# Weight blocks' transfers on GpSimd's queue, and an earlier "free" time in the planner of a two-layer hybrid decoder

## The chip, the cores and the metric

The kernel runs on one core of a Trainium2 chip. Such a core has a matrix engine (TensorE, PE in the profile; PEld is its loading of weights), a vector engine (VectorE, DVE), a scalar engine (ScalarE, ACT), GpSimd (POOL) and SyncE (SP), which here only issues transfers. Each engine has its own program and runs it in order; engines wait for each other at semaphores. Sixteen DMA engines move data between DRAM and the on-chip memory (SBUF); an engine that issues a transfer goes on at once, unless the transfer's own semaphores hold it. The metric is the time of one execution in microseconds on the device, the median of several; lower is better.

## The reference

Two layers, 528 tokens (16 learned meta tokens and 512 real ones), width 1024, float32. Each layer is a mixer and a feed-forward part:

```python
u = rms_norm(h, pre_g)
z = einsum("bld,de->ble", u, w_in)              # q, k, v, forget gate, conv value/gate, sc_b, sc_c, sc_x
y_attn = forgetting_attention(q, k, v, log_f)   # 8 heads of 64, causal softmax with summed log gates
a = causal_depthwise_conv(a_val * sigmoid(a_gate), a_dw_w) + a_dw_b      # 31 taps, 256 channels
y_conv = einsum("blc,ce->ble", silu(layer_norm(a)), a_pw_w)
y_sc = sc_b * causal_depthwise_conv(sc_c * sc_x, sc_conv_w)              # 3 taps, 256 channels
y = head_rms_norm(concat[y_attn, y_conv, y_sc], head_g)
h = h + rms_norm(y @ w_out, post_g)

z = causal_depthwise_conv(rms_norm(h, pre_g) @ w_up, conv_w)             # width 2 x 2816
g, up = split(z)
h = h + rms_norm((silu(g) * up) @ w_down, post_g)
```

The output is h without the meta tokens.

## The kernel before

Tokens lie along the free axis, in two halves of 264 columns; channels lie on 128 partitions, so that h is 8 tiles of 128 x 528. Matrix products keep float32's accuracy by splitting each operand into a high and a low part of a faster format: `mm3` (line 658) issues three matmuls per product, high x high, low x high and high x low. Each weight block, 128 x 1024 as a rule, is therefore loaded raw from DRAM (line 610, 512 KB), rounded to its high part on ACT (line 614), and its low part is the difference on DVE (line 618). There are three raw buffers and a few rings of buffers for the parts. Some weight blocks of layer 1 are prepared during the feed-forward part of layer 0: their parts are written to DRAM (`split_w`), and later fetched as a pair of transfers, high and low (line 626).

The stages are the front (norm of the input and the first half of layer 0's first projection), the mixer of each layer, and each sub-layer's end. Inside a mixer, the projections (`proj`, with the split input uhi and ulo, line 1852 and on), the attention of eight heads and the two convolution branches are interleaved. For a pair of heads, scores are first taken for their row maxima (line 1389, DVE reduces them, line 1396), the maxima go as an extra row into q (line 1416), scores are computed again (line 1435), ACT takes the exponential p (line 1444), POOL zeroes the part above the diagonal (`affine_select`, line 1451), DVE sums (line 1460), and `weighing` (line 1481) multiplies by the values. Odd heads need q and k on other partitions; these are small copies between SBUF tiles issued on SP by the helper `dma` at line 525, as are forget-gate sums through DRAM (`g_dram`, into rows of k).

The convolution branch (tiles apad, cacc) has 31 taps on DVE (line 974), a norm over channels, silu, and a pointwise product (a_pw_w). The short branch (cxp, sccx) has three taps. Each 128-channel tile of the concatenated result then has a head norm: ACT squares it (line 1157), a matmul with a block-diagonal matrix (bd) sums the squares (line 1163), ACT makes the reciprocal root (lines 1128, 1131, 1132), DVE refines it (1133, 1136) and scales (1147), ACT casts the high part (1150) and DVE forms the low one (1151). The output projection with w_out follows; its sums go out at line 1680 with the squares of the next norm at line 746. In the front, the norm's factors rs and rz come from squares (line 746), sums on DVE (755), a matmul (795), ACT (805 to 809) and DVE (810, 816); DVE scales h with them at line 1848.

What sets the order of all this is a planner, `Flow`. Every operation is entered with its engine, an estimated time (0.17 + 0.0009 n us on ACT, 0.17 + 0.00101 n on DVE for n columns; transfers by their bytes), a priority, the operations that it waits for and the buffers that it takes. `Flow.run` walks through a planned time: it takes, again and again, the engine or TensorE thread that can start first, emits its instruction, and sets when that engine is free and when the result is there. So the order of the instructions of each engine, TensorE's matmuls included, is the order in which the plan reaches them. The weight loads are such operations on the engine "sp", whose planned queue they share with the small copies. The inner stretch of the feed-forward part is written without the planner, with loads of its own on SP (lines 473, 494 and 499).

Of the kernel before, what the change touches and what calls it, by code (L numbers as in the profile page):

```python
# [9 lines left out]
F32 = mybir.dt.float32  # L10
# [5 lines left out]
P = 128  # L16
# [19 lines left out]
FIRST = {"w_out": 4, "ffn_w_down": 6}  # L36
# [12 lines left out]
LATE = 6  # L49

WARM, WARM_US = 20, 5.6


_COLS = {}
# [49 lines left out]
def chunk_cols(c):  # L104
    return sum(n for _, n in c[4])
# [102 lines left out]
class Flow:  # L208
# [59 lines left out]
    def run(self, stop=None):  # L268
        while True:
            if stop is not None and stop():  # L270
                return
            best = None
            for eng, ops in self.pend.items():
                can = [(r + self.HOP, o) for o in ops if (r := self.ready(o[4], o[7])) is not None]
                if can:
                    start = max(self.free[eng], min(r for r, _ in can))
                    o = min((o[0], r, o[1], o) for r, o in can if r <= start)[3]
                    if o[0] >= self.yields:
                        soon = [(r, q[0], q[1], q) for r, q in can if q[0] < o[0] - 0.5 and r < start + 0.6 * o[2]]
                        if soon:  # L280
                            start, _, _, o = min(soon)
                    if best is None or start < best[0]:
                        best = (start, eng, o)
            can = [(r, i) for i, t in enumerate(self.threads) if (r := self.ready(t[1])) is not None]
            if can:
                start = max(self.pe, min(r for r, _ in can))
                if best is None or start < best[0]:
                    best = (start, None, self.threads[min(i for r, i in can if r <= start)])
            if best is None:
                assert not self.threads and not any(self.pend.values()), "nothing can go on"  # L290
                return
            start, eng, o = best
            self.now = start
            if eng is not None:
                self.pend[eng].remove(o)
                _, _, us, fn, _, tok, lat, _, takes = o
                for r, slot in takes:
                    r.take(slot)
                fn()
                self.free[eng] = start + us  # L300
                tok.time = start + us + lat
                continue
            self.pe = max(self.pe, start)
            try:
                y = next(o[0])
            except StopIteration:
                self.threads.remove(o)
                continue
            o[1] = [Tok(0.0)] if y is None else [Tok(self.pe + y)] if isinstance(y, float) else y
# [7 lines left out]
def act_us(n):  # L317
    return 0.17 + 0.0009 * n


def dve_us(n):
    return 0.17 + 0.00101 * n


def stt_us(n):
    return 0.22 + 0.00102 * n


def dma_us(n):

    return max(0.35, n * P * 4 / 400e3)


def dma_lat(n):

    return 1.0 + 0.00234 * n
# [3 lines left out]
def tile_hybrid_trunk(ctx: ExitStack, tc: tile.TileContext, xT, wflat, pv_d, out):  # L340
    nc = tc.nc
# [3 lines left out]
    def T(pool, shape, dt, tag, bufs=None):  # L345
        uid[0] += 1
        kw = {} if bufs is None else {"bufs": bufs}
        return pool.tile(list(shape), dt, tag=tag, name=f"{tag}_{uid[0]}", **kw)
# [70 lines left out]
    flow = Flow()  # L419
# [23 lines left out]
    offs = []  # L443
# [13 lines left out]
    def wtile(i, tag):  # L457
        if chunks[i][0] == "a_pw_w":
            if tag == "whi":
                pw_place[0] = pw_place[0]()  # L460
            n = chunks[i][3] * chunk_cols(chunks[i])
            return pw_place[0][:, :n] if tag == "whi" else pw_place[0][:, n:2 * n]
        return T(wx[0], [P, WCHUNK], F32R, tag) if i in wide else T(wp, [P, CHUNK], F32R, tag)
# [19 lines left out]
    for i in ahead:  # L483
        sz = chunks[i][3] * chunk_cols(chunks[i])
# [30 lines left out]
    def act(us, fn, *after, **kw):  # L515
        return flow.op("act", us, fn, after, **kw)

    def dve(us, fn, *after, **kw):
        return flow.op("dve", us, fn, after, **kw)
# [53 lines left out]
    raws = Ring(3)  # L573
    split = {"rot": Ring(3), "wide": Ring(WIDE), "pw": [Ring(1) for _ in range(DEPTH)]}
    coming = deque()
    fetched, filled = [], []
# [18 lines left out]
    def plan_w(limit, prio=2):  # L595

        for i in range(wpos[0], min(limit, len(chunks))):
            plan_block(i, prio)
        wpos[0] = max(wpos[0], min(limit, len(chunks)))

    def plan_block(i, prio):
        kn, n = chunks[i][3], chunk_cols(chunks[i])
        sz = kn * n
        b = Block()
        box = {}
        slot = Slot()

        def load():
            box["raw"] = T(wp, [P, CHUNK], F32, "raw", 3)
            nc.sync.dma_start(box["raw"][:, :sz], wflat[offs[i]:offs[i] + P * sz].rearrange("(p s) -> p s", p=P))  # L610

        def high():
            box["hi"] = wtile(i, "whi")
            nc.scalar.copy(box["hi"][:, :sz], box["raw"][:, :sz])  # L614

        def low():
            lo = wtile(i, "wlo")
            nc.vector.tensor_sub(lo[:, :sz], box["raw"][:, :sz], box["hi"][:, :sz].bitcast(F32))  # L618
            b.w = tuple(t[:, :sz].rearrange("p (k n) -> p k n", n=n) for t in (box["hi"], lo))

        ring = split["pw"][chunks[i][1]] if chunks[i][0] == "a_pw_w" else split["wide" if i in wide else "rot"]
        if i in home:
            def fetch():
                ws = wtile(i, "whi"), wtile(i, "wlo")
                for t, d in zip(ws, (home[i][0], home[i][1])):
                    nc.sync.dma_start(t[:, :sz].bitcast(F32), d[:, :sz])
                b.w = tuple(t[:, :sz].rearrange("p (k n) -> p k n", n=n) for t in ws)

            b.tok = flow.op("sp", 2 * dma_us(sz), fetch, filled, prio=prio, lat=dma_lat(sz), takes=[(ring, b.slot)])
            fetched[:] = [b.tok]  # L630
            coming.append((i, b))
            return

        got = flow.op("sp", dma_us(sz), load, prio=prio, lat=dma_lat(sz), takes=[(raws, slot)])
        a = act(act_us(sz), high, got, *fetched, prio=prio, takes=[(ring, b.slot)])
        filled[:] = [a]
        b.tok = dve(dve_us(sz), low, a, prio=prio)
        slot.close(b.tok)
        coming.append((i, b))
# [27 lines left out]
    def two(t):  # L667
        return t.rearrange("p (a b) -> p a b", a=2)
# [1143 lines left out]
    with tc.tile_pool(name="pre", bufs=2, reuse_waits="tile") as sp, tc.manual_schedule(engines=every):  # L1812
# [13 lines left out]
        for k in range(KD):  # L1826
# [3 lines left out]
            d = dve(stt_us(H), lambda hk=hk, hi=hi, lo=lo, gc=gc: nc.vector.scalar_tensor_tensor(  # L1830
                lo, in0=hk, scalar=gc, in1=hi.bitcast(F32), op0=ALU.mult, op1=ALU.subtract), c, prio=0)
# [46 lines left out]
    for l in range(DEPTH):  # L1878
# [21 lines left out]
        with tc.tile_pool(name=f"fp{l}", bufs=2, reuse_waits="tile") as fp:  # L1900
# [78 lines left out]
            for part, nf in enumerate(PARTS):  # L1979
# [14 lines left out]
                if part < len(PARTS) - 1:  # L1994
                    for m in range(KD):
                        w = next_w()
                        ps = mmt()
                        if final:

                            mm3({0: ps[:, 0, :2 * fw]}, w, ks, lambda b, k, hf, f0=f0: g[f0 + k][b][:, :2 * fw])  # L2000
                            d, src = yp[:, m, t0:], ps[:, 0, :2 * fw]
                        else:
                            mm3({hf: ps[:, hf, :fw] for hf in range(2)}, w, ks, grhs)
                            d, src = two(yp[:, m, t0:]), ps[:, :, :fw]
# [69 lines left out]
```

## Time and profile before

| | us |
|---|---|
| median of 3 runs | 1304.11 |
| lowest, highest | 1301.64, 1304.61 |
| the profiled execution, its own time | 1301.54 |
| its span in the trace | 1299.8 |
| ACT busy | 612.6 (47%) |
| small groups left out of the page, busy | 1424.2 |

The profile has 24250 instructions. The granted clock of TensorE has a mean of 0.995 of full speed. Busy time is a sum over instructions of an engine; a row of waits names the instruction that waited and what released it last. Matmuls overlap in TensorE's pipeline: a single one lasts longer in the trace than the distance to the next. A row such as `L658` is the line of the kernel before; `SPq` and `POOLq` are the issuing of transfers by those engines.

### The profile page before, as it was taken

The page shows a single profiled execution, that of the slowest core. Times are in us where ns is not written, and L with a number is a line of the kernel's source. Part 1 is how long each engine was busy: PE and PEld are TensorE (multiplying, and loading weights), DVE is VectorE, ACT ScalarE, POOL GpSimd, SP SyncE. Part 2 cuts the span into 40 slices and gives each one's busy share as a digit, 9 for nine tenths or more (in the row PEclk, how much of TensorE's full clock was granted, in tenths as well). Part 3 has the DMA queues.
Part 4 walks back from the last instruction along what each step waited for, and adds up shares of the span by engine and source line. Part 5 has one row for each costly group of instructions (what it writes and reads, how often), then busy time and mean ns, then how long its engine had stood idle before and what let it go on. Part 6 is the DMA issues. An engine that isn't in the chain of part 4 may idle for free. (4 is left out here: it accounts for less than half of the span.)

```text
span 1299.8 us, 24250 instructions
## 1 busy us (share of the span) xinstructions
PE 1273.3 (98%) x9922; PEld 1217.7 (94%) x9922; DVE 895.1 (69%) x1563; ACT 612.6 (47%) x1144; POOL 58.8 (5%) x166
## 2 busy tenths in 40 slices
PE   8999999999999999999999899999999999999997
PEld 8988888999999999999999798889999799989997
DVE  7888896688734774677568786756876256636664
ACT  7255567655433442444552344676543234314453
POOL 1310100000000000000003111100000000000000
PEclk9999999999999999999999999989999999999999
DMA  7032213516554556654742353234033323232321
GB/s 238 34 101 84 81 54 101 190 56 205 203 173 157 192 199 223 227 195 146 241 158 68 116 164 123 74 118 145 18 98 97 97 85 94 72 116 91 92 72 65
DMA packets 56335, 164.56 MB, mean 127 GB/s; under 512 B 6352, under 2 KB 16720, under 8 KB 56224
## 3 DMA queue, kind: packets, MB, share of 16 engines
q1 hardware_dynamic: 56176, 162.88, 38.7%
q8 instruction: 78, 1.28, 0.4%
q14 instruction: 33, 0.27, 0.1%
q0 software_dynamic: 48, 0.13, 0.0%
HBM read 131.17 MB, written 27.46 MB: 122 GB/s over the span
## 5 line engine op out<-in xcount | busy, mean ns | idle before, releaser
L658 PE MATMUL psum<-uhi,whi 128*128 128x264 f32 (+1 forms) x1936 | 452.8, 287 | 1.3 <-ACT uhi L1852 0.8
L658 PE MATMUL psum<-ulo,whi 128*128 128x264 f32 (+1 forms) x1936 | 445.5, 284 | 0.6 <-DVE ulo L1854 0.4
L658 PE MATMUL psum<-uhi,wlo 128*128 128x264 f32 (+1 forms) x1936 | 445.2, 284 | 0.0
L658 PEld LDWEIGHTS psum<-uhi,whi 128*128 128x128 f32 x1936 | 322.8, 189 | 3.9 <-ACT uhi L1852 1.0
L658 PEld LDWEIGHTS psum<-ulo,whi 128*128 128x128 f32 x1936 | 322.4, 188 | 1.9 <-DVE ulo L889 0.6
L658 PEld LDWEIGHTS psum<-uhi,wlo 128*128 128x128 f32 x1936 | 322.7, 189 | 0.0
L658 PE MATMUL psum<-yhi,whi 128*128 128x264 f32 (+3 forms) x888 | 250.4, 305 | 6.4 <-ACT yhi L1150 2.1
L658 PE MATMUL psum<-ylo,whi 128*128 128x264 f32 (+3 forms) x888 | 247.6, 301 | 1.0 <-DVE ylo L1151 1.0
L658 PE MATMUL psum<-yhi,wlo 128*128 128x264 f32 (+3 forms) x888 | 247.6, 301 | 0.8 <-DVE wlo L618 0.8
L475 ACT CAST whi<-raw 128x1024 fp32r<-128x1024 f32 (+1 forms) x110 | 113.1, 1030 | 182.9 <-PE psum L658 145.0
L476 DVE TENSOR_TENSOR wlo<-raw,whi 128x1024 fp32r<-128x1024 f32 (+1 forms) x110 | 131.7, 1199 | 65.5 <-ACT whi L475 63.7
L658 PEld LDWEIGHTS psum<-yhi,whi 128*128 128x128 f32 x888 | 160.8, 191 | 15.1 <-ACT yhi L1150 3.5
L658 PEld LDWEIGHTS psum<-ylo,whi 128*128 128x128 f32 x888 | 161.0, 190 | 7.5 <-DVE ylo L1151 1.9
L658 PEld LDWEIGHTS psum<-yhi,wlo 128*128 128x128 f32 x888 | 161.2, 190 | 6.7 <-DVE wlo L618 1.4
L1955 DVE SCALAR_TENSOR_TENSOR c<-z,pv,c 128x528 f32<-128x528 f32 (+1 forms) x176 | 131.9, 756 | 2.7
L618 DVE TENSOR_TENSOR wlo<-raw,whi 128x1024 fp32r<-128x1024 f32 (+2 forms) x64 | 75.6, 1196 | 28.0 <-ACT whi L614 27.7
L974 DVE SCALAR_TENSOR_TENSOR cacc<-apad,pv,cacc 128x528 f32<-128x528 f32 x120 | 87.5, 763 | 1.0
L614 ACT CAST whi<-raw 128x1024 fp32r<-128x1024 f32 (+2 forms) x64 | 64.7, 1028 | 25.9 <-PE psum L658 15.1
L1965 ACT ACTIVATE c<-c 128x528 f32<-128x528 f32 (+1 forms) x44 | 28.1, 639 | 83.7 <-DVE c L1955 83.6
L1973 ACT CAST yhi<-c 128x528 fp32r<-128x528 f32 (+1 forms) x44 | 27.5, 626 | 84.2 <-DVE c L1969 84.2
L1953 ACT ACTIVATE c<-z,pv 128x528 f32<-128x528 f32 (+1 forms) x88 | 63.4, 727 | 0.1
L1921 DVE TENSOR_TENSOR z<-psum,rz 128x250 f32<-128x250 f32 x80 | 30.4, 420 | 46.5 <-PE psum L658 46.4
(220 smaller groups left out, 1424.2 us busy)
## 6 DMA issues: line engine op xcount, KB each, us to landing
raw<-in_w_dram SPq DMA_DIRECT2D x160, 512.0 KB
raw<-in_w_dram SPq DMA_DIRECT2D x32, 448.0 KB
split_w<-whi SPq DMA_DIRECT2D x20, 512.0 KB
split_w<-wlo SPq DMA_DIRECT2D x20, 512.0 KB
whi<-split_w SPq DMA_DIRECT2D x20, 512.0 KB
wlo<-split_w SPq DMA_DIRECT2D x20, 512.0 KB
h<-in_x_dram SPq DMA_DIRECT2D x16, 264.0 KB
q<-q SPq DMA_DIRECT2D x16, 132.0 KB
```

The source lines that it names most:

```text
L475: nc.scalar.copy(hi[:, :sz], raw[:, :sz])
L476: nc.vector.tensor_sub(lo[:, :sz], raw[:, :sz], hi[:, :sz].bitcast(F32))
L614: nc.scalar.copy(box["hi"][:, :sz], box["raw"][:, :sz])
L618: nc.vector.tensor_sub(lo[:, :sz], box["raw"][:, :sz], box["hi"][:, :sz].bitcast(F32))
L658: nc.tensor.matmul(d, lhsT=w[a][:, k, cols], rhs=rhs(b, k, hf), start=start and i == 0 and p == 0, stop=stop and i == n - 1 and p == 2)
L974: nc.vector.scalar_tensor_tensor(conv[j], in0=src, in1=conv[j], scalar=col("a_dw_w", CK * j + i), op0=ALU.mult, op1=ALU.add)
L1921: nc.vector.tensor_mul(t[:, off + a - i0:off + z - i0], src, rz[:, a:z])
L1953: nc.scalar.activation(dst, src[:, 2:2 + 2 * fw], AF.Copy, scale=wtap(2, t))
L1955: nc.vector.scalar_tensor_tensor(dst, in0=src[:, i:i + 2 * fw], scalar=wtap(i, t), in1=dst, op0=ALU.mult, op1=ALU.add)
L1965: silu = nc.scalar.activation(cs[0], cs[0], AF.Silu)
L1973: nc.scalar.copy(ghi, cs[0])
```

## The change

Three things change. First, the transfers of all weight blocks from block 6 on (both the raw loads and the fetched pairs, in both layers' planned stages) are issued by GpSimd, on a planned engine of their own, "wdma"; each pushes the planner's free time of "pool" on by 0.75 us. The first six raw loads, the small copies, the loads of h and the feed-forward part's own loads stay on SP. Of the issues, 104 change their engine: 60 raw loads and 44 halves of fetched pairs. Second, the raw loads on the new queue wait in the plan for the last load on SP (`behind`). Third, after an operation the planner sets its engine free 0.09 us earlier than the operation's estimated end (for operations under 0.18 us, at half of it); transfers' queues are left out of this, and the time at which a result is there stays as it was. The lines behind the change are numbered higher, by 1 at first, by 11 around line 620, and by 13 from line 650 on (so line 1451 becomes 1464, and 1163 becomes 1176).

```diff
--- before.py
+++ after.py
@@ -49,6 +49,7 @@
 LATE = 6
 
 WARM, WARM_US = 20, 5.6
+GP_DMA = 0.75
 
 
 _COLS = {}
@@ -297,7 +298,7 @@
                 for r, slot in takes:
                     r.take(slot)
                 fn()
-                self.free[eng] = start + us
+                self.free[eng] = start + (us if eng in ("sp", "wdma") else max(us - 0.09, 0.5 * us))
                 tok.time = start + us + lat
                 continue
             self.pe = max(self.pe, start)
@@ -598,16 +599,26 @@
             plan_block(i, prio)
         wpos[0] = max(wpos[0], min(limit, len(chunks)))
 
+    behind = []
+
     def plan_block(i, prio):
         kn, n = chunks[i][3], chunk_cols(chunks[i])
         sz = kn * n
         b = Block()
         box = {}
         slot = Slot()
+        queue = "wdma" if i >= FIRST["ffn_w_down"] else "sp"
+
+        def bring(to, src):
+            if queue == "sp":
+                nc.sync.dma_start(to, src)
+                return
+            flow.free["pool"] = max(flow.free.get("pool", 0.0), flow.now) + GP_DMA
+            nc.gpsimd.dma_start(to, src)
 
         def load():
             box["raw"] = T(wp, [P, CHUNK], F32, "raw", 3)
-            nc.sync.dma_start(box["raw"][:, :sz], wflat[offs[i]:offs[i] + P * sz].rearrange("(p s) -> p s", p=P))
+            bring(box["raw"][:, :sz], wflat[offs[i]:offs[i] + P * sz].rearrange("(p s) -> p s", p=P))
 
         def high():
             box["hi"] = wtile(i, "whi")
@@ -623,15 +634,17 @@
             def fetch():
                 ws = wtile(i, "whi"), wtile(i, "wlo")
                 for t, d in zip(ws, (home[i][0], home[i][1])):
-                    nc.sync.dma_start(t[:, :sz].bitcast(F32), d[:, :sz])
+                    bring(t[:, :sz].bitcast(F32), d[:, :sz])
                 b.w = tuple(t[:, :sz].rearrange("p (k n) -> p k n", n=n) for t in ws)
 
-            b.tok = flow.op("sp", 2 * dma_us(sz), fetch, filled, prio=prio, lat=dma_lat(sz), takes=[(ring, b.slot)])
+            b.tok = flow.op(queue, 2 * dma_us(sz), fetch, filled, prio=prio, lat=dma_lat(sz), takes=[(ring, b.slot)])
             fetched[:] = [b.tok]
             coming.append((i, b))
             return
 
-        got = flow.op("sp", dma_us(sz), load, prio=prio, lat=dma_lat(sz), takes=[(raws, slot)])
+        got = flow.op(queue, dma_us(sz), load, behind if queue == "wdma" else (), prio=prio, lat=dma_lat(sz), takes=[(raws, slot)])
+        if queue == "sp":
+            behind[:] = [got]
         a = act(act_us(sz), high, got, *fetched, prio=prio, takes=[(ring, b.slot)])
         filled[:] = [a]
         b.tok = dve(dve_us(sz), low, a, prio=prio)
```

The order of SP's issues in the mixer of layer 1, where the copies of the odd heads' q and k are made (q and k are copies between tiles, whi and wlo the fetched pair of a weight block), was:

```order
L525 DMA q_767_7988<-q_766_7987 64x528
L525 DMA q_769_7990<-q_768_7989 64x528
L626 DMA whi_8305<-split_w_114 128x1024
L626 DMA wlo_8306<-split_w_114 128x1024
L626 DMA whi_8336<-split_w_114 128x1024
L626 DMA wlo_8337<-split_w_114 128x1024
L525 DMA k_759_7980<-k_758_7979 64x528
L525 DMA k_761_7982<-k_760_7981 64x528
L626 DMA whi_8450<-split_w_114 128x1024
L626 DMA wlo_8451<-split_w_114 128x1024
```

and is now, at the same copies:

```order
L526 DMA q_767_7990<-q_766_7989 64x528
L526 DMA q_769_7992<-q_768_7991 64x528
L526 DMA k_759_7982<-k_758_7981 64x528
L526 DMA k_761_7984<-k_760_7983 64x528
L526 DMA k_758_7981<-g_dram_21_113 1x528 x2
L526 DMA k_760_7983<-g_dram_21_113 1x528 x2
L526 DMA q_771_7994<-q_770_7993 64x528
L526 DMA q_773_7996<-q_772_7995 64x528
```

The fetched pairs are gone from between the copies, which follow each other. On POOL, in the same mixer, what stands between the last clearing of buffers and the first causal selects (p, a head's exponentials) is now:

```order
L617 DMA whi_8176<-split_w_114 128x1024
L617 DMA wlo_8177<-split_w_114 128x1024
L617 DMA whi_8212<-split_w_114 128x1024
L617 DMA wlo_8213<-split_w_114 128x1024
L617 DMA whi_8269<-split_w_114 128x1024
L617 DMA wlo_8270<-split_w_114 128x1024
L617 DMA whi_8344<-split_w_114 128x1024
L617 DMA wlo_8345<-split_w_114 128x1024
L1464 AFFINE_SELECT p_776_8015<-p_776_8015 128x128 x4
L1464 AFFINE_SELECT p_776_8015<-p_776_8015 16x16
L617 DMA whi_8472<-split_w_114 128x1024
L617 DMA wlo_8473<-split_w_114 128x1024
```

Before, the selects followed the clearing with no transfer between them; now four pairs stand ahead of the first select, and a fifth pair between those of two heads.

At the end of the mixer of layer 0 TensorE's rows from the last two sums of squares of the head norms (L1163; apad holds squares of the convolution branch, yhi and ylo are the normed tiles that the output projection reads) were:

```order
L1163 MATMUL psum_67<-apad_2666,bd_93 128x264
L1163 MATMUL psum_67<-apad_2665,bd_93 128x264
L658 MATMUL psum_67<-yhi_292_2681,whi_2238 128x264
L658 MATMUL psum_67<-ylo_293_2682,whi_2238 128x264
L658 MATMUL psum_67<-yhi_292_2681,wlo_2299 128x264
L658 MATMUL psum_67<-yhi_292_2681,whi_2432 128x264
L658 MATMUL psum_67<-ylo_293_2682,whi_2432 128x264
L658 MATMUL psum_67<-yhi_292_2681,wlo_2471 128x264
L658 MATMUL psum_67<-yhi_294_2693,whi_2238 128x264
L658 MATMUL psum_67<-ylo_295_2694,whi_2238 128x264
L658 MATMUL psum_67<-yhi_294_2693,wlo_2299 128x264
L658 MATMUL psum_67<-yhi_294_2693,whi_2432 128x264
```

and from the last two sums of squares now (L1176; cxp holds squares of the short branch):

```order
L1176 MATMUL psum_67<-cxp_2650,bd_93 128x264
L671 MATMUL psum_67<-yhi_140_1156,whi_2262 128x264
L671 MATMUL psum_67<-ylo_141_1157,whi_2262 128x264
L671 MATMUL psum_67<-yhi_140_1156,wlo_2269 128x264
L671 MATMUL psum_67<-yhi_140_1156,whi_2515 128x264
L671 MATMUL psum_67<-ylo_141_1157,whi_2515 128x264
L671 MATMUL psum_67<-yhi_140_1156,wlo_2545 128x264
L1176 MATMUL psum_67<-cxp_2650,bd_93 128x264
L671 MATMUL psum_67<-yhi_158_1357,whi_2262 128x264
L671 MATMUL psum_67<-ylo_159_1358,whi_2262 128x264
L671 MATMUL psum_67<-yhi_158_1357,wlo_2269 128x264
L671 MATMUL psum_67<-yhi_158_1357,whi_2515 128x264
```

Before, the convolution branch's norms came last, and the matmuls right behind the last sums read their result: the first use of a second half of it is the thirteenth matmul. Now the short branch's norm is last, and tiles with finished norms are read first: between the first of the two sums and the first use of its tile (yhi_297) are 42 matmuls of the output projection, between the second and its use 78.

In the front, ACT's rows from the second half's norm factor (rs) to the first casts of the scaled input (uhi; sccx and cxp are the gates of the convolution branch here, whi a weight block) were:

```order
L805 ACTIVATE rs_47_176<-psum_67,c_rms_101 128x264
L808 ACTIVATE rs_47_176<-rs_47_176 128x264
L809 ACTIVATE rs_47_176<-rs_47_176 128x264
L935 ACTIVATE sccx_140<-sccx_140 128x264
L935 ACTIVATE cxp_144<-cxp_144 128x264
L937 ACTIVATE sccx_140<-sccx_140,c_one_99 128x264
L937 ACTIVATE cxp_144<-cxp_144,c_one_99 128x264
L938 ACTIVATE sccx_140<-sccx_140 128x264
L938 ACTIVATE cxp_144<-cxp_144 128x264
L1852 CAST uhi_106<-h_175 128x2x264
L614 CAST whi_437<-raw_340 128x1056
L1852 CAST uhi_106<-h_175 128x2x264 x5
```

and are now:

```order
L818 ACTIVATE rs_47_176<-psum_67,c_rms_101 128x264
L821 ACTIVATE rs_47_176<-rs_47_176 128x264
L948 ACTIVATE sccx_140<-sccx_140 128x264
L822 ACTIVATE rs_47_176<-rs_47_176 128x264
L950 ACTIVATE sccx_140<-sccx_140,c_one_99 128x264
L1865 CAST uhi_106<-h_175 128x2x264
L951 ACTIVATE sccx_140<-sccx_140 128x264
L948 ACTIVATE cxp_144<-cxp_144 128x264
L1865 CAST uhi_106<-h_175 128x2x264
L950 ACTIVATE cxp_144<-cxp_144,c_one_99 128x264
L625 CAST whi_415<-raw_331 128x1056
L1865 CAST uhi_106<-h_175 128x2x264
```

The casts of uhi now begin among the gates' rows, and the weight block's cast stands behind the second of them.

## The prediction

> **What bounds the kernel now.** I read the page's busy shares first, then the busy time in windows of 50 us, then TensorE's waits, then the timeline around each wait that is longer than a third of a microsecond.
>
> ```profile
> PE 1273.3 (98%) x9922; PEld 1217.7 (94%) x9922; DVE 895.1 (69%) x1563; ACT 612.6 (47%) x1144; POOL 58.8 (5%) x166
> ```
>
> TensorE (PE) is busy for 1273.3 of 1299.8 us, so all that a change of order and of queues can win is its 26.5 us of idle time. No matmul is added or taken away by the diff. The windows (stretch, its length, then busy us and instructions of PE, weight load, DVE, ACT, POOL, the granted clock, the DMA share, GB/s) show where the idle time lies:
>
> ```profile
> 200.00:250.00 50.00, 47.33 (x366) 45.42 (x365) 28.68 (x48) 33.06 (x70) 0.27 (x4) 1.00 0.47 149
> 350.00:400.00 50.00, 50.00 (x412) 50.00 (x411) 18.29 (x20) 16.37 (x23) 0.00 (x0) 1.00 0.44 141
> 700.00:750.00 50.00, 45.01 (x352) 40.41 (x351) 38.19 (x93) 17.27 (x50) 4.39 (x12) 0.97 0.38 122
> 850.00:900.00 50.00, 48.16 (x359) 45.98 (x359) 28.18 (x47) 31.92 (x64) 0.00 (x0) 0.93 0.49 156
> ```
>
> The feed-forward part (350 to 400) has no idle time: one matmul per 50 / 412 = 0.121 us. Only the mixers and their ends lose time: 2.67 us in 200 to 250, 4.99 in 700 to 750, 1.84 in 850 to 900. TensorE's waits (us in total, times, longest) name what came last:
>
> ```profile
> PE psum L1435 <- DMA k<-k: 3.5, 1, 3.5
> PE psum L658 <- ACT yhi L1150: 2.1, 2, 1.5
> PE psum L658 <- ACT whi L614: 2.0, 1, 2.0
> ...
> PE psum L658 <- DVE ylo L1151: 1.0, 3, 0.4
> ...
> PE psum L1435 <- ACT q L1416: 0.9, 1, 0.9
> PE psum L658 <- ACT uhi L1852: 0.8, 1, 0.8
> ...
> PE psum L658 <- ACT acc L746: 0.5, 1, 0.5
> ...
> PE psum L658 <- DVE ulo L1854: 0.4, 1, 0.4
> ```
>
> The longest is a small copy of one head's keys. The next three kinds are the head norms at the end of a mixer (L1150, L1151), and the first weight block, which stays on SP and which I leave at 2.0. Weight transfers are otherwise hidden.
>
> **The change part by part.** *The keys' copy, mixer 1.* These are SP's issues ahead of it, PE's matmul that waited, and the sizes:
>
> ```profile
> 718.73 0.55 SPq L626 DMA_DIRECT2D whi<-split_w  x1
> ...
> 720.33 0.39 SPq L626 DMA_DIRECT2D wlo<-split_w  x1
> 720.82 1.36 SPq L525 DMA_DIRECT2D k<-k  x2
> ```
> ```profile
> 728.70 1.21 PE L1435 MATMUL psum<-q,k 128*128 128x16 f32 x5 [3.54 <-DMA k<-k]
> ```
> ```profile
> whi<-split_w SPq DMA_DIRECT2D x20, 512.0 KB
> ...
> k<-k SPq DMA_DIRECT2D x16, 132.0 KB
> ```
>
> Four transfers of 512 KB stand directly ahead of two of 132 KB, and the matmul that needs the first copy starts at 728.70, 7.9 us after its issue. These 2.3 MB in the 10 us from 718.73 to 728.70 are some 230 GB/s: the copy waited behind weights. In the new order SP holds nothing but small copies there, and the four fetches stand on POOL. If the copies no longer queue behind 2 MB, they land 2 to 4 us after issue (an estimate: their own 0.26 MB at 230 GB/s is 1.1 us, and the one transfer on POOL's queue, row below, took 4.0 with its fixed part); PE had been ready 3.54 us before 728.70, which is 4.3 us after the issue. Bounds: 0 if the engines still serve them in order of issue, 3.5 if not, and below nothing if they get worse, which I exclude since the bytes around them are the same. I take **3.5**, nearest to the 4.3 us of room. The rule that speaks against it is in the Trainium skill, "DMA: Bandwidth & Descriptors", section "Issuing engines are not separate DMA queues": DMAs of all issuers run on the same 16 engines and interleave, so that another issuer saves only the time to issue. By it the 3.5 would shrink towards nothing; its section "Queues, rings and completion order" has each engine alternate between queue rows packet by packet, by which a short copy would take its half share and pass. No run here shows two rows at once, so both stay.
>
> *The end of each mixer.* PE's, then ACT's rows around the last head norm of mixer 0, then PE's waits in mixer 1:
>
> ```profile
> 213.91 1.05 PE L1163 MATMUL psum<-apad,bd 128*128 128x264 f32 x4
> ...
> 215.68 0.39 PE L658 MATMUL psum<-ylo,whi 128*128 128x264 f32 x1 [0.38 <-DVE ylo L1151]
> ...
> 218.39 0.41 ACT L1150 CAST yhi<-cacc 128x264 fp32r<-128x264 f32 x1 [0.94 <-DVE cacc L1147]
> ...
> 218.85 0.51 PE L658 MATMUL psum<-yhi,whi 128*128 128x264 f32 x2 [1.48 <-ACT yhi L1150]
> ```
> ```profile
> 860.41 1.52 PE L1163 MATMUL psum<-apad,bd 128*128 128x264 f32 x4 [0.61 <-DVE rs_t L1133]
> ...
> 862.83 0.43 PE L658 MATMUL psum<-ylo,whi 128*128 128x250 f32 x1 [0.39 <-DVE ylo L1151]
> ...
> 866.01 0.81 PE L658 MATMUL psum<-yhi,whi 128*128 128x264 f32 x2 [0.62 <-ACT yhi L1150]
> ```
>
> From the end of the last statistics matmul (213.91 + 1.05 = 214.96) to the cast of its result (218.39 + 0.41) are 3.8 us. In the old order 12 matmuls, 1.5 us at 0.121, stand between those matmuls and the first that uses a second half; hence the waits. In the new order the convolution's pointwise product and norm come before the short convolution's, and the last norm's first half has 42 output-projection matmuls (5.1 us) and its second 78 (9.4 us) before their use. 5.1 and 9.4 both exceed 3.8, the first by only 1.3, which two extra ACT rows in between take up. Gain: 0.38 + 1.48 + 0.3 (the two smaller waits in mixer 0 have 1.0 in three with mixer 1's 0.39 and 0.38) = 2.1, and 0.61 + 0.39 + 0.62 = 1.6 in mixer 1: **3.7**, bounds 2 and 4.5. The 0.5 for acc L746, a wait for a PSUM buffer to be read out, I leave.
>
> *The opening.* PE's two waits, and ACT's rows before them:
>
> ```profile
> 31.01 0.39 PE L658 MATMUL psum<-uhi,whi 128*128 128x264 f32 x1 [0.77 <-ACT uhi L1852]
> 31.77 0.39 PE L658 MATMUL psum<-ulo,whi 128*128 128x264 f32 x1 [0.37 <-DVE ulo L1854]
> ```
> ```profile
> 26.14 0.41 ACT L935 ACTIVATE sccx<-sccx 128x264 f32<-128x264 f32 x1
> 26.45 0.41 ACT L935 ACTIVATE cxp<-cxp 128x264 f32<-128x264 f32 x1
> ...
> 28.21 0.62 ACT L1852 CAST uhi<-h 128x528 fp32r<-128x528 f32 x1
> ...
> 30.32 0.63 ACT L1852 CAST uhi<-h 128x528 fp32r<-128x528 f32 x1 [0.52 <-DVE h L1848]
> ```
>
> Six small rows (26.14 to 28.21) and a weight cast stand ahead of the first two casts of u; in the new order the first cast follows two of them, that weight cast comes behind the second cast of u, and DVE scales three tiles of h ahead of the second half's factor instead of none. I count both waits as gone: **1.1**, bounds 0 and 1.1, since the earlier norm matmuls may wait 0.2 to 0.4 themselves.
>
> *Restart.* After a wait PE's next matmul starts later than 0.121 us behind (31.01 shows 0.39 of one matmul, against 0.28 to 0.29 in a running stream), some 0.1 for each of the ten waits counted: **1.0**.
>
> *The planner's rule.* The two L935 rows start 0.31 us apart though each lasts 0.41: an engine really starts the next operation some 0.1 before the end of one. The old plan spaces such a row at 0.17 + 0.0009 x 264 = 0.41, the new one at 0.32. So the new plan is near the chip and without slack; where an operation starts later than planned, PE has less work placed ahead. I put **1.5 back** (some ten dense places of the mixers at 0.15, the 0.1 of a row and a half), bounds 0 and 10 (ten at the 1.0 of the larger waits above).
>
> *POOL's queue.* 104 issues (60 raw loads, 44 halves of prepared blocks) move to POOL. These rows are POOL's group for its one old transfer and its landing, its causal selects, its own waits, DVE's waits for the selects, and SP's for a free block:
>
> ```profile
> L378 POOL DMA_DIRECT2D pv<-in_pv_dram x1 | 0.7, 668 | 0.8 <-POOLq L2065 0.8
> ```
> ```profile
> pv<-in_pv_dram POOLq DMA_DIRECT2D x1, 127.0 KB, 4.0
> ```
> ```profile
> L1451 POOL TENSOR_SCALAR_AFFINE_SELECT p<-p 128x128 f32<-128x128 f32 (+1 forms) x80 | 30.1, 388 | 234.9 <-ACT p L1444 234.0
> ```
> ```profile
> POOL p L1451 <- ACT p L1444: 234.0, 43, 31.9
> ...
> ACT whi L614 <- DMA raw<-in_w_dram: 10.1, 12, 2.0
> ...
> DVE psum L1460 <- POOL p L1451: 6.2, 10, 3.2
> ```
>
> At 0.668 us, 104 issues are 69 us on an engine busy for 58.8 of 1299.8: no load of its own. Both have 128 rows of one partition each, so I take 0.668; were the time to grow with bytes it would be 512 / 127 x 0.668 = 2.7 us each, 280 us in all. What matters is order: behind a weight transfer that waits for its buffer stand the next causal selects, and behind those DVE's sums and PE's weighing. The selects waited 234 us in 43 waits for ACT, some 5 us each, which covers an issue pair (1.3); in ten cases DVE waited for the select, and there a pair is not covered. I take **0**, since the plan places each transfer where its buffer should be free; bounds −1 and 14 (fourteen places of the order have a weight transfer right ahead of selects, at 1 us).
>
> **Sum.** 3.5 + 3.7 + 1.1 + 1.0 − 1.5 = 7.8 us against the profiled run of 1301.54 (its span 1299.8): 1293.7. The median is 2.6 above that run, so on its terms 1304.11 − 7.8 = 1296.3; I say 1296.
>
> **Rivals.**
> - *The copy stays late* (the 16 engines serve the old queue of bytes anyway). For: the copy needs bandwidth that the fetches still use. Against: it was issued last and landed last. Without 3.5 and 0.1 the sum is 4.2: 1300.
> - *Only the issue moves, and the tight plan returns what it wins.* For: weights were hidden but for 2.0, and the new plan has no slack. Against: the waits above are waits of order. Payback 8 instead of 1.5: 1302 to 1305.
> - *POOL in order blocks attention (slower).* A transfer on POOL waits for its buffer, or takes 2.7 us to write, and the selects behind it come late for PE's weighing. It decides when a delay exceeds the some 5 us that selects waited on the mean; in the worst places eight issues stand ahead of the first selects, 5.3 us at 0.668 but 21 at 2.7. At 1 us for each of 14 places the 7.8 turns to −6: 1310. Against: ACT is what selects wait for.
> - *Descriptors starved by DVE.* If POOL's issue had to wait for a running DVE operation, 1.2 us later landings would show in ACT's 12 waits for raw blocks (2.0 at most now), and little on PE: 1297 to 1303. The Trainium skill, "SBUF — State Buffer", its warning on DVE blocking DMAs of GpSimd, has descriptors held up while DVE runs a copy in its two-port mode; the DVE rows here are two-input operations, so that I give it little.
>
> **How the numbers follow.** Forecast 0.57; copy stays late 0.12; plan returns it 0.13; POOL blocks 0.13; starved 0.05. The range takes the forecast with its bounds (1290 if nothing is paid back and the 0.9 wait for ACT q L1416 and others go too) up to the second rival's end and part of the third: 1290 to 1307. Two runs of this kernel can be told apart by about 0.2%, 2.6 us: faster is the forecast, the late copy and half of the starved case, 0.71; same 0.14; slower 0.15.
>
> **What would show it.** Right: no DMA k<-k among PE's waits of mixer 1; no wait for the head norm's cast and difference (new lines 1163 and 1164, old 1150 and 1151) at a mixer's end; POOL's issues near 0.67 us. Wrong: POOL waiting at a transfer just ahead of selects while PE waits for them in the weighing (new line 1494, old 1481); a mean issue far above 0.67; new waits of 0.5 to 1 us at the pointwise product or the score matmuls; or PE's idle time near 26 us as before.

## The result, and the profile after

The changed kernel takes 1317.17 us (median of 4, 1316.08 to 1319.29) against 1303.23 (1301.64 to 1304.61) for the kernel before: a ratio of 1.0113 with a 95% interval of 1.0101 to 1.0125. It is slower by some 14 us, where 1296 was forecast and the range ended at 1307. The profiled execution took 1316.85 us, its span is 1315.1.

The page's busy shares of after, and four of the windows that were read before:

```profile
PE 1281.2 (97%) x9922; PEld 1221.7 (93%) x9922; DVE 893.9 (68%) x1563; ACT 612.5 (47%) x1144; POOL 113.4 (9%) x270
```
```profile
200.00:250.00 50.00, 46.39 (x339) 44.46 (x338) 29.04 (x53) 32.25 (x70) 4.98 (x13) 0.93 0.38 128
350.00:400.00 50.00, 50.00 (x412) 50.00 (x411) 26.75 (x32) 20.29 (x27) 0.00 (x0) 1.00 0.55 184
700.00:750.00 50.00, 48.51 (x386) 45.67 (x384) 46.85 (x107) 14.32 (x41) 18.05 (x41) 1.00 0.37 118
850.00:900.00 50.00, 46.12 (x360) 43.32 (x357) 30.14 (x57) 33.05 (x75) 4.25 (x8) 0.97 0.38 122
```

The span grew by 15.3 us in two ways. TensorE is idle for 33.9 us (1315.1 less 1281.2) instead of 26.5: 7.4 more. And the same 9922 matmuls keep it busy for 7.9 us longer. The granted clock, the third number from the end, says most of why: over the span its mean is 0.990, where it was 0.995, and at 200 to 250 it is 0.93, where it was 1.00. At 700 to 750 and 850 to 900 it is higher than before. The feed-forward part is as before.

TensorE's waits of after (some of the longest groups; add 13 to a line of before, 11 around line 620):

```profile
PE psum L1176 <- DVE rs_t L1146: 4.1, 2, 2.0
PE psum L671 <- ACT whi L625: 2.9, 1, 2.9
PE psum L1402 <- ACT yta L1524: 1.8, 1, 1.8
PE psum L1402 <- DVE mcol L1409: 1.4, 3, 0.7
...
PE psum L1176 <- DVE sccx L1088: 1.2, 2, 0.6
PE psum L671 <- DVE cxp L1072: 1.1, 2, 0.5
```

The copy of k is gone from the list, and so are the two waits of the opening (uhi L1852 and ulo L1854). In their place are many waits for VectorE, led by two of 2.0 us at the sums of squares of a head norm. (The 2.9 for whi is the first weight block, at the start, 2.0 before.) Where the time is lost shows in the first start of a scores matmul of layer 1 (all instructions of that line from 700 to 800 us; name and count, durations, first and last start), before and after:

```profile
L1389 PE MATMUL psum<-k,q x36: 170/300/480, 719.4 to 796.3; 128*128 128x264 f32 x12, 128*16 128x16 f32 x6, 128*128 128x144 f32 x6, 128*128 128x272 f32 x6
```
```profile
L1402 PE MATMUL psum<-k,q x30: 172/313/451, 734.0 to 796.9; 128*128 128x264 f32 x10, 128*16 128x16 f32 x5, 128*128 128x144 f32 x5, 128*128 128x272 f32 x5
```

Layer 1's attention starts 14.6 us later, so that nearly all of the 15.3 us is lost in layer 0. A finer measure is the time at which the n-th matmul starts, of the 9922 in each trace. By it after is 6.6 us behind before at before's 164 us, 7.8 at 186, 11.1 at 228 and 14.2 at 303: about half of layer 0's loss lies ahead of the end of its mixer. In layer 1 it is 14.4 us behind ahead of the copy of k, 10.4 behind it (734 us), 16.0 at 827 and 15.3 at the end. So what is won at the copy is lost again in the attention that follows.

The worst single place of layer 0 is the end of its mixer. TensorE's rows for the sums of squares, and windows of 2 us around them:

```profile
210.87 1.13 PE L1176 MATMUL psum<-apad,bd 128*128 128x264 f32 x4 [0.62 <-DVE sccx L1088]
...
214.04 1.25 PE L1176 MATMUL psum<-apad,bd 128*128 128x264 f32 x2 [2.04 <-DVE rs_t L1146]
```
```profile
210.00:212.00 2.00, 1.38 (x7) 0.72 (x5) 1.64 (x4) 0.97 (x3) 0.00 (x0) 1.00 0.62 225
212.00:214.00 2.00, 0.00 (x0) 0.00 (x0) 0.92 (x3) 1.94 (x7) 0.00 (x0) 0.79 0.00 0
214.00:216.00 2.00, 1.96 (x7) 1.66 (x8) 1.95 (x6) 1.06 (x3) 0.00 (x0) 0.50 0.00 0
216.00:218.00 2.00, 2.00 (x11) 2.00 (x11) 1.56 (x5) 1.38 (x5) 0.00 (x0) 0.50 0.00 0
218.00:220.00 2.00, 2.00 (x11) 2.00 (x11) 0.05 (x1) 0.00 (x0) 0.00 (x0) 0.50 0.00 0
220.00:222.00 2.00, 2.00 (x17) 1.93 (x17) 1.47 (x3) 1.72 (x4) 0.00 (x0) 1.00 0.00 0
```

In the order of after, four such sums (two tiles, two halves; the profile has each as two matmuls) stand within 13 TensorE rows, before the short branch's. They take their PSUM banks from a ring of two (`banks["mm"]`), which they share with the projections. A bank comes free only when its sums have been read: the second waits 0.62 us for a projection's (sccx, L1088), the third uses the first one's bank, and the fourth waits 2.04 us until VectorE has read the second's for the reciprocal root (L1146). The plan has the same wait: printed while the kernel is written out, it lets TensorE stand 2.07 us at the fourth sum. So this is no surprise to the planner, but a matter of the order that it came to. Behind that the granted clock is 0.50 for over 6 us, in which a window of 2 us holds 11 matmuls instead of 17.

VectorE's rows a little earlier in layer 0 show the second thing:

```profile
107.49 0.76 DVE L987 SCALAR_TENSOR_TENSOR cacc<-apad,pv,cacc 128x528 f32<-128x528 f32 x1
108.28 0.87 DVE L1363 TENSOR_TENSOR k<-psum,k 64x264 fp32r<-64x264 f32 x2
109.19 0.77 DVE L987 SCALAR_TENSOR_TENSOR cacc<-apad,pv,cacc 128x528 f32<-128x528 f32 x1
109.99 0.43 DVE L1146 SCALAR_TENSOR_TENSOR rs_t<-psum,rs_t 128x264 f32<-128x264 f32 x1
110.34 0.76 DVE L987 SCALAR_TENSOR_TENSOR cacc<-apad,pv,cacc 128x528 f32<-128x528 f32 x1
```

The last row starts at 110.34, 0.08 before the end of the one ahead of it (109.99 + 0.43). The second starts 0.03 behind it (107.49 + 0.76 = 108.25), as do the third and fourth. The planner's 0.09 us is true of the first kind alone. Counted over all VectorE rows from 80 to 215 us, 171 start on an overlap (0.078 us in the mean), 48 start 0 to 0.06 us after the end, and 52 wait longer. From 80 to 140 us VectorE is busy for 56.0 of 60 us, so that what the plan takes for free there must be made up by later work.

### The profile page after: what moved, and what is told of

Its sections match the earlier page's. It is cut to its first block, busy times and chain, and to the rows that moved or that the text cites. A ratio compares the mean times of both kernels' runs of the same rounds, so it can differ in the third digit from the quotient of the medians.

```text
span 1315.1 us, 24327 instructions
## 1 busy us (share of the span) xinstructions
PE 1281.2 (97%) x9922; PEld 1221.7 (93%) x9922; DVE 893.9 (68%) x1563; ACT 612.5 (47%) x1144; POOL 113.4 (9%) x270
## 5 line engine op out<-in xcount | busy, mean ns | idle before, releaser
L671 PE MATMUL psum<-uhi,whi 128*128 128x264 f32 (+1 forms) x1936 | 458.9, 289 | 2.6 <-DVE rs_t L1146 1.0
L671 PE MATMUL psum<-ulo,whi 128*128 128x264 f32 (+1 forms) x1936 | 451.0, 285 | 0.5 <-DVE ulo L902 0.5
L671 PE MATMUL psum<-uhi,wlo 128*128 128x264 f32 (+1 forms) x1936 | 450.4, 285 | 0.0
L671 PEld LDWEIGHTS psum<-uhi,whi 128*128 128x128 f32 x1936 | 326.2, 190 | 6.1 <-DVE rs_t L1146 2.1
L671 PEld LDWEIGHTS psum<-ulo,whi 128*128 128x128 f32 x1936 | 325.8, 189 | 1.9 <-DVE ulo L902 1.0
L671 PEld LDWEIGHTS psum<-uhi,wlo 128*128 128x128 f32 x1936 | 326.1, 190 | 0.0
L617 POOL DMA_DIRECT2D raw<-in_w_dram x60 | 32.1, 534 | 960.6 <-DVE wlo L477 708.7
```

The source lines that it names most:

```text
L617: nc.gpsimd.dma_start(to, src)
L671: nc.tensor.matmul(d, lhsT=w[a][:, k, cols], rhs=rhs(b, k, hf), start=start and i == 0 and p == 0, stop=stop and i == n - 1 and p == 2)
```

## The experiments

Theory R: the planner's rule is the cause. Theory Q: GpSimd's queue is (the slower rival of the prediction).

**e1** takes the kernel before with the rule alone; **e2** the changed kernel with the old rule.

```diff
e1, on the kernel before:
-                self.free[eng] = start + us
+                self.free[eng] = start + (us if eng == "sp" else max(us - 0.09, 0.5 * us))
e2, on the changed kernel:
-                self.free[eng] = start + (us if eng in ("sp", "wdma") else max(us - 0.09, 0.5 * us))
+                self.free[eng] = start + us
```

> The kernel before with the planner's new rule alone; all weight transfers stay on SP. Theory R (the rule: an operation that waits for the one before it on its engine starts 0.03 us after its end in the trace of after, one that does not 0.08 us before it; the rule counts the 0.09 for all, so the plan runs ahead of the chip where VectorE is full): 1312 to 1322 us, with TensorE waits of 0.5 to 2 us at the pointwise product and the head norms of mixer 0. Theory Q (GpSimd's queue delays the causal selects or the weights): 1296 to 1304, since nothing is on that queue.

> The changed kernel with the planner's old rule; only the weight blocks' transfers move to GpSimd. Theory R: 1294 to 1302 us: no wait for the copy of k in mixer 1 (3.5 us) and no stretch of half clock behind it (1.7), the rest as before. Theory Q: 1314 to 1320, all of the slowdown.

e1 took 1314.87 us (ratio 1.0091, 1.0076 to 1.0106), e2 1302.01 (0.9990, 0.9981 to 1.0000). The rule alone makes nearly the whole slowdown, the queue alone none: Q falls. But the queue alone is not as fast as R expected either, at the edge of its range. In e2's trace the wait for the copy is gone (by matmuls done, 3.7 us behind before ahead of the copy, 1.6 ahead of it behind), and the win is lost again from 808 to 846 us, where e2 falls to 4.1 behind, in part by a wait that before has not:

```profile
PE psum L671 <- DVE sccx L1088: 2.5, 1, 2.5
```

**e3** has half the cut, **e5** the full cut for VectorE alone, **e4** for ScalarE alone.

```diff
e3:
-max(us - 0.09, 0.5 * us)
+max(us - 0.045, 0.5 * us)
e5 (e4: "act"):
-(us if eng in ("sp", "wdma") else max(us - 0.09, 0.5 * us))
+(max(us - 0.09, 0.5 * us) if eng == "dve" else us)
```

> The changed kernel with 0.045 us in place of 0.09 in the rule, about the mean of the 171 overlapped and 48 waiting starts on VectorE in mixer 0 (0.078 x 171 - 0.03 x 48, over 219, is 0.054). Theory R: between the two, 1296 to 1308 us. Theory Q: 1314 to 1320, as with the full cut.

> The changed kernel with the rule for VectorE alone; ScalarE and GpSimd keep the old one. Theory R with VectorE as the engine that falls behind: most of the slowdown stays, 1308 to 1318 us. If ScalarE's share is what does it: 1294 to 1303. Theory Q: 1314 to 1320.

> The changed kernel with the rule for ScalarE alone; VectorE keeps the old one. If each engine's cut costs its own part (VectorE's alone took 1302.0 of the queue alone to 1309.0, both 1317.2): 1306 to 1313 us. If ScalarE's cut only hurts beside VectorE's: 1298 to 1304.

e3 took 1297.11 us (0.9952, 0.9937 to 0.9967): faster than the kernel before. e5 took 1309.04 (1.0042, 1.0028 to 1.0057), e4 1302.24 (0.9990, 0.9980 to 0.9999). So a cut on ScalarE alone costs nothing against e2's 1302.0, and VectorE's costs 7; the parts do not add, since the full rule costs 15. (It covers GpSimd's own operations too, which neither part has; these were not tried alone.)

**e8** asks for the queue's worth at a plan that fits: the kernel before with a cut of 0.045 and all transfers on SP, to be held against e3.

> The kernel before with the rule at 0.045 us, all transfers on SP. If the queue gives its part once the plan fits (3.5 us wait for the copy of k and 1.7 us of half clock): 1300 to 1305 us against the 1297.1 with the queue. If the queue gives nothing: 1295 to 1299.

e8 took 1302.76 us (0.9995, 0.9986 to 1.0005), 5.7 more than e3. The two are alike up to the start of layer 1's scores (722.1 and 722.2 us), and e8 has in its waits what e3 has not, and behind it a slower clock (1.00 in both windows in e3):

```profile
PE psum L1435 <- DMA k<-k: 2.3, 1, 2.3
```
```profile
730.00:734.00 4.00, 2.83 (x15) 2.62 (x16) 0.95 (x6) 1.18 (x3) 0.58 (x2) 0.81 0.02 7
734.00:740.00 6.00, 6.00 (x43) 5.55 (x43) 4.07 (x15) 3.55 (x10) 0.77 (x3) 0.84 0.51 175
```

With the queue, SP issues the two copies by themselves. In after they are these, and no TensorE wait names them:

```profile
733.87 1.10 SPq L526 DMA_DIRECT2D k<-k  x2
```

**e6** and **e7** ask how the rule does harm: by results that are expected too early, or by an engine that is planned too full. e6 adds slack at every hand-off; e7 takes the cut from the evictions of q and k, which are those that start late most often.

```diff
e6:
-    HOP = 0.06
+    HOP = 0.15
e7, in both evictions and in the rule (shortened):
+                    a.keep = d.keep = True
-(us if eng in ("sp", "wdma") else
+(us if eng in ("sp", "wdma") or hasattr(tok, "keep") else
```

> The changed kernel with 0.15 us in place of 0.06 as the planner's hand-off from one operation to one that waits for it; the 0.09 cut stays. Theory O (occupancy: the plan packs an engine denser than it runs): stays slow, 1310 to 1320 us. Theory S (slack: only the hand-offs are planned too early): 1297 to 1306.

> The changed kernel, but the eviction of q and k (high part on ScalarE, low part on VectorE, 64 x 264 each; in the trace of after 41 of 52 on VectorE and 29 of 42 on ScalarE start 0 to 0.06 us after the end of the one before, not 0.08 before it) keeps its full planned time; all else keeps the cut. Theory O: about half of the slowdown goes, 1301 to 1310 us. Theory S: 1313 to 1320.

e6 took 1303.20 us (1.0000, 0.9991 to 1.0010), e7 1313.27 (1.0079, 1.0063 to 1.0094). By what was set down both lie in the range of slack, e7 at its lower edge; yet e7 takes 3.9 us from after, clear of noise, so that the evictions' time has a part, and e6's other times give another order as well. Neither theory is shown by these two. This is the planner's own clock, printed while a kernel is written out, beside the chip's, up to the end of layer 0's planned work:

| kernel | planned, us | on the chip, us | chip less plan |
|---|---|---|---|
| before (no cut) | 294.5 | 284.0 | -10.5 |
| e2 (no cut, queue) | 294.1 | 287.7 | -6.4 |
| e9 (0.0225) | 291.0 | 288.8 | -2.2 |
| e3 (0.045) | 288.5 | 288.6 | +0.1 |
| e6 (0.09, more hand-off) | 285.8 | 288.2 | +2.4 |
| e10 (0.0675) | 282.9 | 288.0 | +5.1 |
| after (0.09) | 287.5 | 301.2 | +13.7 |

Plans without a cut are late against the chip, those with the full cut early; the two meet at a cut of 0.045. From 80 to 140 us the plan fills VectorE to 0.96 or 0.97 in before and after alike, and the chip takes about 0.05 us less than the uncut estimate for each operation: 53.2 us against 58.4 over 104 operations in before, 57.2 against 62.6 over 109 in after (planned sums from that print, the chip's from busy time and gaps of up to 0.06 us). But the difference doesn't order the times: with the chip 5.1 us behind its plan e10 is as fast as e3 (below).

**e9**, **e10** and **e11** follow the size of the cut: 0.0225, 0.0675, and 0.05 on VectorE with 0.058 on ScalarE.

> The changed kernel with 0.0225 us in the rule. From the stretch 80 to 140 us, where the plan fills VectorE to 0.96 or 0.97: the chip needs 0.05 us less for an operation than the uncut estimate, before (58.4 planned, 53.2 on the chip, 104 operations) as after (62.6 uncut, 57.2 on the chip, 109). Theory O: as long as the cut stays below 0.05 the chip keeps up with the plan: 1296 to 1302 us, between 1302.0 without a cut and 1297.1 at 0.045. If the order that a cut happens to give decides, and not its size: anywhere from 1295 to 1312.

> The changed kernel with 0.0675 us in the rule. Theory O: above 0.05 the plan packs VectorE denser than it runs, some 0.018 us for each of its operations, against 0.04 at 0.09: 1302 to 1311 us, with the chip 1 to 4 us behind the plan in the mixer of layer 0. If the order decides: anywhere from 1295 to 1315.

> The changed kernel with the cut that the trace gives for each engine: 0.05 us on VectorE, 0.058 on ScalarE (37.1 uncut less 32.2 on the chip, over 83 operations). Theory O: as good as 0.045 for both: 1294 to 1300 us. If the order decides: anywhere from 1295 to 1312.

They took 1296.37 us (0.9951, 0.9936 to 0.9967), 1296.60 (0.9951, 0.9936 to 0.9966) and 1302.56 (0.9999, 0.9989 to 1.0009). e10 and e11 both miss: 0.0675 should have been slow and the fitted cut fast. By the planner's clock e11 is on time (290.5 us planned, 290.4 on the chip) and slow all the same. So the size of the cut isn't all; the order that a plan happens to give counts too. Of the plans, those of after, e1 and e7, and of e11, have in layer 0 the four sums of squares within 13 rows and the short branch's behind them; after and e7 have it in layer 1 too. e11's waits there are longer still (its plan has them too, with 1.93 and 3.79 us):

```profile
205.83 1.14 PE L1176 MATMUL psum<-apad,bd 128*128 128x264 f32 x2 [2.31 <-DVE rs_t L1146]
...
209.83 1.25 PE L1176 MATMUL psum<-apad,bd 128*128 128x264 f32 x2 [2.85 <-DVE rs_t L1146]
```

**e12** and **e13** therefore give these sums other banks, in the changed kernel and in e11; **e14** does e7 and e12 together, and **e15** puts the banks on e9.

```diff
-                ps, slot = yield from bank("mm")
+                ps, slot = yield from bank("acc" if i in (4, 5) else "mm")
                 nc.tensor.matmul(ps[:, :H], lhsT=bd, rhs=sq[:, half_sl(hf)], start=True, stop=True)
```

> The changed kernel (cut 0.09), but the sums of squares of the convolution branch's head norms take their PSUM banks from the attention's output ring, not from the two of the projections; the plan is the same up to the first of these sums in layer 0. Theory B (the sums wait 2.0 us in each mixer for a bank, and TensorE's clock halves behind it, 3.4 us lost at 212 to 220 and 1.7 at 868 to 872): 1305 to 1312 us, without the waits for rs_t of 4.1 us. Theory O alone (VectorE behind the plan; the wait only moves to the next use): 1314 to 1318.

> e11 (0.05 and 0.058 us) with the same change of banks. Theory B: its waits of 2.3 and 2.9 us in layer 0 go and the time falls from 1302.6 to 1294 to 1299 us, level with 0.0225, 0.045 and 0.0675. If the waits only move: 1301 to 1304.

> The changed kernel with both edits of e7 and e12: evictions of q and k at their full planned time, and other banks for the convolution branch's sums of squares. If the two causes add (9.0 and 4.0 us): 1302 to 1306 us. If they are one (VectorE late at the end of the mixer is what made the banks late): 1306 to 1309, as e12.

> e9 (cut 0.0225) with the change of banks. e9's wait for a bank is 0.3 us. If the change of banks only removes a pile-up: 1295 to 1298 us, level with e9's 1296.4. If it gains by itself: below 1293.

e12 took 1308.14 us (1.0040, 1.0025 to 1.0055), 9.0 less than after; e13 1298.48 (0.9962, 0.9948 to 0.9976), 4.1 less than e11. Both waits are gone. e12's windows at the place shown above:

```profile
212.00:214.00 2.00, 2.00 (x17) 1.97 (x16) 1.68 (x5) 1.56 (x5) 0.00 (x0) 1.00 0.00 0
214.00:216.00 2.00, 2.00 (x17) 1.93 (x16) 1.23 (x4) 2.00 (x7) 0.00 (x0) 1.00 0.00 0
216.00:218.00 2.00, 2.00 (x17) 1.94 (x17) 2.00 (x5) 1.64 (x4) 0.00 (x0) 1.00 0.00 0
218.00:220.00 2.00, 2.00 (x19) 2.00 (x18) 1.74 (x5) 1.82 (x6) 0.53 (x1) 1.00 0.00 0
```

From 212 to 220 us there are 70 matmuls in e12 and 29 in after, at a clock of 1.00 instead of 0.50 from 214 on. By matmuls done, e12 wins 4.9 us in layer 0 and 3.8 in layer 1. e14 took 1303.97 (1.0010, 1.0001 to 1.0019), 4.2 less than e12, as e7 had taken 3.9 from after: the two causes add. e15 took 1293.64 (0.9933, 0.9916 to 0.9950), 2.7 less than e9, between the two answers set down for it; it is the fastest of all, 0.7% below the kernel before. As e9's wait for a bank was 0.3 us, the change of banks gains by the order that follows from it as well, and the 9.0 of e12 may hold some of that.

## Why the prediction was wrong, step by step

- **The keys' copy: right in effect, wrong in how it comes about.** 3.5 us were taken, and the wait is gone in after; e3 against e8 gives 5.7 for the queue. At the copy e8 loses 4.0 of these, its wait of 2.3 and 1.7 by the clock (4 x 0.19 + 6 x 0.16, above); the rest lies further on, where the two orders differ. The prediction left the clock out though the 0.97 and 0.93 stood in its windows. In before the clock halves behind the wait for k:

```profile
730.00:732.00 2.00, 2.00 (x12) 1.93 (x10) 0.97 (x5) 0.57 (x2) 0.58 (x2) 0.50 0.00 0
732.00:734.00 2.00, 2.00 (x14) 1.86 (x13) 0.79 (x3) 1.21 (x5) 0.56 (x3) 0.67 0.14 18
```

  That is 2 x 0.5 + 2 x 0.33 = 1.7 us. But the copies don't land "2 to 4 us after issue". By the packets in the traces (2112 bytes each), the last one of the two copies ends 7.7 us after the first is issued in before and 7.5 in e8, and still 6.2 in e3 and 6.5 in after, beside a pair that GpSimd issues within half a microsecond of them. In e3 they are there 2.8 us sooner than in e8: 1.5 because SP has no four transfers to issue ahead of them (722.02 instead of 723.49), and 1.3 by a shorter way. So the rival by which the copy stays late was not far off: the wait went by a margin of 0.45 us (last packet at 728.26, first of the matmuls at 728.71). In e3 one pair is on the way beside the copies, in e8 two are ahead of them: what the second queue does by itself was not tried.
- **The end of each mixer: this step failed.** "5.1 and 9.4 both exceed 3.8" counted the matmuls behind the last norm, and 3.7 us as won. These waits, for the head norm's cast and difference, are gone in after. But the step didn't look at the norm that moved ahead: its four sums came close together on two banks. After has 5.3 us of waits there in its two mixers (4.1 for rs_t, 1.2 for sccx), and half clock behind them, 3.0 us at 214 to 220 and 1.7 at 868 to 872; e12 puts the change of banks at 9.0 us. The count of the moved step's own matmuls and of the banks they hold was missing.
- **The planner's rule: right in sign, wrong in size by far.** "I put 1.5 back", where after takes 15.2 us more than e2, from which it differs by the rule alone. The step took an operation's early start, seen in one pair of rows, for a property of all. Of VectorE's starts that didn't wait long, 48 of 219 had no overlap. The full cut against 0.045 costs 20 us (1317.2 less 1297.1): 9.0 by the banks and 4.2 more by the evictions of q and k (e14), both outside this term's ten places of 0.15. The remaining 6.9 us, from e14's 1304.0 to 1297.1, have no experiment; by matmuls done e14 is 1.7 us behind e3 at 734 us and 5.9 at 827, so that most of them arise in layer 1's attention. That a plan ahead of the chip is the cause is shown for none of the three: the banks' wait stands in the plan itself, and with 0.0675 e10 is as fast as e3.
- **The opening: right.** Its two waits (1.1 us) are gone.
- **Restart: too small.** 1.0 us was taken for slow restarts; the half clock behind the sums of squares of layer 0 alone costs 3 x 2 x 0.5 = 3.0, by the windows of 2 us from 214 to 220 above (ahead of 214 no matmul ran that it could slow).
- **POOL's queue: right at 0, as far as e3 shows.** An issue takes less than the 0.668 taken, and the longest waits on this row are for a raw buffer outside the mixers:

```profile
L617 POOL DMA_DIRECT2D raw<-in_w_dram x60 | 32.1, 534 | 960.6 <-DVE wlo L477 708.7 <-DVE wlo L629 192.6 <-ACT apad L1170 28.0
```
```profile
DVE psum L1473 <- POOL p L1464: 8.7, 12, 2.9
```

  VectorE waits 8.7 us for the selects against 6.2 before, while e3, e9 and e10, with the same queue and 3.2, 8.4 and 8.4 us of these waits, are faster than the kernel before. The slower rival had the sign right but another cause. The second rival, that the tight plan returns what it wins, comes nearest, with 8 us where some 22 were lost (1317.2 less 1294.8, the forecast without its 1.5); but what it names, missing slack, does not explain the banks.

## What to carry to other kernels

A planner's times decide an order, and a small change of them gives another order. Fitting the cost of an operation to what full stretches of the trace show in the mean was not enough here (e11): measure several values, since neighbouring ones differed by 6 us, and read the plan itself for waits that it knows of. When a step moves, count the buffers and PSUM banks that its instructions hold in the new place as well as the work that hides it. A queue of its own for bulk transfers paid here where a short urgent copy stood behind them, and in e2 another order lost the win again further on.

## What the runs showed that was not expected

The granted clock falls to 0.50 behind waits much shorter than the 3.5 us of before: at 214 us in after, behind 2.04 us, and it stays there for over 6 us. With its aftermath a wait costs nearly twice what the list of waits says here: 9.0 us by e12 for 5.3 of waits. The Trainium skill, "TensorE: Matmul & The Clock Gate", Part 1: The HAM clock gate, has the clock drop after an idle window of about 3.4 us; here one idle stretch of 2.04 us with four matmuls and 0.62 us of waiting ahead of it was enough. And an engine overlaps the start of an instruction with the end of the last (0.08 us on VectorE) in most cases only: of the 64 evictions of q and k on VectorE in after, 52 start 0 to 0.06 us after the end of the one ahead, 4 on an overlap, and 8 wait longer. Laid beside the program, the trace shows what the late ones have in common. 105 VectorE instructions of after begin, with an input or their output, at another group of 32 partitions than the last one that read or wrote the same memory (57 of the 64 evictions are such), and none of them overlaps; all 881 starts with an overlap stay at the same group. No run changes this alone, so that it is not shown as the cause, but a planner could price it.
